# Which engine ends the program: the last wait for HBM copies moves from GpSimd to SyncE

## The chip, the cores and the metric

The kernel runs on one core of a Trainium2 chip. The metric is device time in microseconds; before the change the median of three runs is 106.08 us (105.78 to 106.34). A profile of one execution (a trace, and a page made from it) is read beside it; that execution took 106.19 us.

## The reference

A token is kept where its position is below the capacity, and set to zero otherwise:

```python
def setup_inputs():
    batch, seq, hidden, capacity = 16, 1024, 512, 256
    return {
        "x": np.random.randn(batch, seq, hidden).astype(np.float32),
        "token_positions": np.random.randint(0, capacity, (batch, seq)).astype(np.int32),
        "capacity": capacity,
    }

def reference(x, token_positions, capacity):
    mask = token_positions < capacity
    return (x * mask[..., np.newaxis]).astype(np.float32)
```

`x` has 16,384 tokens of 512 float32 numbers, 33.55 MB. The positions reach the chip as 64-bit integers, and the kernel reads them as pairs of 32-bit words. With these inputs every position lies below the capacity, so no token is dropped and the output equals `x`.

## The kernel before

The kernel bets that nothing is dropped, and repairs the output if something was.

**The copies.** Lines 77 to 83 issue eight copies from `x` to `out`, HBM to HBM, of 4 MB each, in turn from SyncE (`sp`) and ScalarE (`act`). Each adds 16 to the semaphore `s_copy` when it has landed, one from each DMA engine, so all eight are done at 128. ScalarE issues the load of the token positions (line 72) ahead of its copies. Lines 86 to 95 then take these nine instructions out of their place and put them at the very start of the program, ahead of the compiler's own opening barriers, so that the copies begin at once.

**The flag.** VectorE compares the positions with the capacity (lines 103 to 117: `ge`, `lt`, `low`, `keep`, each 128 x 128), adds up each row (`kept`, line 119), TensorE adds the rows (line 123), and line 125 makes the flag `drop_i`: 1 if fewer than all tokens are kept. SyncE, ScalarE and VectorE read it into a register (line 133). If it is 1, lines 141 to 161 load all of `x` in blocks through two buffers, multiply by `keep` on VectorE and write over the copies, after waiting for `s_copy`. With these inputs the flag is 0 and the three engines jump over that part.

**The end.** Semaphores have to be at zero for the next launch. SyncE, ScalarE and VectorE each add 1 to `s_done` as they leave (lines 164 and 165; the trace files these under line 165). GpSimd (`gp`) has nothing to do until here: it waits until `s_done` is 3 (line 166), clears the range of all semaphores but `s_copy` (line 170), then waits for all eight copies (line 171) and sets `s_copy` back by 128 (line 172). Lines 171 and 172 become one instruction. It is the last of the program, and the only one that makes sure that the copies have landed.

The order of the work is written out by hand; each engine runs its own list of instructions, and nothing but semaphores ties them together. What an engine does after its last instruction of the program belongs to the runtime, not to the kernel.

Of the kernel before, what the change touches and what calls it, by code (L numbers as in the profile page):

```python
# [1 line left out]

# [4 lines left out]


@with_exitstack
def kernel(  # L10
    ctx: ExitStack,
    tc: tile.TileContext,
    x: bass.AP,
    token_positions: bass.AP,
    capacity: bass.AP,
    out: bass.AP,
):
    nc = tc.nc
    P = nc.NUM_PARTITIONS
    fp32 = mybir.dt.float32  # L20
    i32 = mybir.dt.int32
    Alu = mybir.AluOpType

    x_f = x.flatten_outer_dims()
    out_f = out.flatten_outer_dims()
    N, D = x_f.shape
    n_per_p = N // P
    cap = float(int(capacity))
    x_r = x_f.rearrange("(p n) d -> p n d", p=P)
    out_r = out_f.rearrange("(p n) d -> p n d", p=P)  # L30
    tp_i32 = token_positions.rearrange("b s -> (b s)").bitcast(i32)

    sp = nc.sync
    act = nc.scalar
    ve = nc.vector
    pe = nc.tensor
    gp = nc.gpsimd


    tc.close()  # L40
    tc.compile()  # L41

    def sbuf(name, shape, dtype):
        return ctx.enter_context(nc.sbuf_tensor(name, shape, dtype)).ap()

    tp = sbuf("tp", [P, 2 * n_per_p], i32)
    ge = sbuf("ge", [P, n_per_p], fp32)
    lt = sbuf("lt", [P, n_per_p], fp32)
    low = sbuf("low", [P, n_per_p], fp32)
    keep = sbuf("keep", [P, n_per_p], fp32)  # L50
    kept = sbuf("kept", [P, 1], fp32)
    ones = sbuf("ones", [P, 1], fp32)
    drop_i = sbuf("drop_i", [1, 1], i32)
    total = ctx.enter_context(nc.psum_tensor("total", [1, 1], fp32)).ap()
    F = 16
    NBUF = 2
    n_fix = n_per_p // F
    xts = [sbuf(f"xt{b}", [P, F, D], fp32) for b in range(NBUF)]

    s_copy = nc.alloc_semaphore("s_copy")  # L60
    s_tp = nc.alloc_semaphore("s_tp")
    s_ve = nc.alloc_semaphore("s_ve")
    s_pe = nc.alloc_semaphore("s_pe")
    s_ld = [nc.alloc_semaphore(f"s_ld{b}") for b in range(NBUF)]
    s_mul = nc.alloc_semaphore("s_mul")
    s_st = [nc.alloc_semaphore(f"s_st{b}") for b in range(NBUF)]
    s_done = nc.alloc_semaphore("s_done")

    n_copy = 0
    early = []  # L70

    load_tp = act.dma_start(out=tp, in_=tp_i32.rearrange("(p w) -> p w", p=P))
    early.append(load_tp.then_inc(s_tp, 16).ins)

    C = 16
    for k in range(n_per_p // C):
        ins = (sp, act)[k % 2].dma_start(
            out=out_r[:, k * C : (k + 1) * C, :], in_=x_r[:, k * C : (k + 1) * C, :]  # L80
        ).then_inc(s_copy, 16)
        early.append(ins.ins)
        n_copy += 1


    home = nc.cur_bb.bb
    first_bb = nc.cur_f.blocks[0]
    first_sp = next(
        k for k, i in enumerate(first_bb.instructions) if i.engine == mybir.EngineType.SP
    )  # L90
    names = [i.name for i in early]
    home.instructions = [i for i in home.instructions if i.name not in names]
    first_bb.instructions = (
        first_bb.instructions[:first_sp] + early + first_bb.instructions[first_sp:]
    )

    lo = tp[:, 0 : 2 * n_per_p : 2]
    hi = tp[:, 1 : 2 * n_per_p : 2]


    ve.memset(ones, 1.0).then_inc(s_ve, 1)  # L101
    ve.wait_ge(s_tp, 16)
    ve.tensor_scalar(  # L103
        out=ge, in0=lo, scalar1=0.0, scalar2=None, op0=Alu.is_ge
    ).then_inc(s_ve, 1)
    ve.wait_ge(s_ve, 2)
    ve.scalar_tensor_tensor(  # L107
        out=lt, in0=lo, scalar=cap, in1=ge, op0=Alu.is_lt, op1=Alu.mult
    ).then_inc(s_ve, 1)
    ve.wait_ge(s_ve, 3)  # L110
    ve.scalar_tensor_tensor(  # L111
        out=low, in0=hi, scalar=0.0, in1=lt, op0=Alu.is_equal, op1=Alu.mult
    ).then_inc(s_ve, 1)
    ve.wait_ge(s_ve, 4)
    ve.scalar_tensor_tensor(  # L115
        out=keep, in0=hi, scalar=0.0, in1=low, op0=Alu.is_lt, op1=Alu.add
    ).then_inc(s_ve, 1)
    ve.wait_ge(s_ve, 5)
    ve.tensor_reduce(  # L119
        out=kept, in_=keep, axis=mybir.AxisListType.X, op=Alu.add  # L120
    ).then_inc(s_ve, 1)
    pe.wait_ge(s_ve, 6)
    pe.matmul(out=total, lhsT=ones, rhs=kept, start=True, stop=True).then_inc(s_pe, 1)  # L123
    ve.wait_ge(s_pe, 1)
    ve.tensor_scalar(  # L125
        out=drop_i, in0=total, scalar1=float(N) - 0.5, scalar2=None, op0=Alu.is_lt
    ).then_inc(s_ve, 1)


    for e in (sp, act, ve):  # L130
        e.wait_ge(s_ve, 7)
    ET = mybir.EngineType
    drop = nc.values_load(
        drop_i[0:1, 0:1],
        engines=[ET.SP, ET.Activation, ET.DVE],
        min_val=0,
        max_val=1,
        skip_runtime_bounds_check_because="a comparison gives 0 or 1",
    )
    with nc.If(drop):  # L140
        for u in range(n_fix):
            b = u % NBUF
            if u >= NBUF:
                sp.wait_ge(s_st[b], 16 * (u // NBUF))
            sp.dma_start(out=xts[b], in_=x_r[:, u * F : (u + 1) * F, :]).then_inc(s_ld[b], 16)
            ve.wait_ge(s_ld[b], 16 * (u // NBUF + 1))
            for j in range(F):
                c = u * F + j
                ve.tensor_scalar(
                    out=xts[b][:, j, :],  # L150
                    in0=xts[b][:, j, :],
                    scalar1=keep[:, c : c + 1],
                    scalar2=None,
                    op0=Alu.mult,
                ).then_inc(s_mul, 1)
            if u == 0:
                act.wait_ge(s_copy, 16 * n_copy)
            act.wait_ge(s_mul, (u + 1) * F)
            act.dma_start(out=out_r[:, u * F : (u + 1) * F, :], in_=xts[b]).then_inc(s_st[b], 16)
        for b in range(NBUF):  # L160
            act.wait_ge(s_st[b], 16 * (n_fix // NBUF))


    for e in (sp, act, ve):
        e.sem_inc(s_done, 1)
    gp.wait_ge(s_done, 3)
    own = [s_tp, s_ve, s_pe, *s_ld, s_mul, *s_st, s_done]
    ids = sorted(s.num for s in own)
    assert ids == list(range(ids[0], ids[-1] + 1))
    gp.sem_clear(range(ids[0], ids[-1] + 1))  # L170
    gp.wait_ge(s_copy, 16 * n_copy)
    gp.sem_inc(s_copy, -16 * n_copy)


# [1 line left out]
_INS = ['x', 'token_positions', 'capacity']  # L176
_OUTS = [((16, 1024, 512), 'float32')]

_NUMBERS = {'capacity': 256}


# [26 lines left out]
```

## Time and profile before

| what | value |
|---|---|
| time, median of three runs | 106.08 us |
| time of the profiled execution | 106.19 us |
| its span, first to last instruction | 104.3 us |
| HBM read, written | 33.69 MB, 33.55 MB |
| both together over the span | 645 GB/s |
| SyncE's queue, ScalarE's queue, share of 16 DMA engines' span | 48.6%, 49.4% |
| VectorE, GpSimd, TensorE busy | 1.5, 0.2, 0.2 us |

The page gives first how long each engine was busy, then the span in 40 equal slices with a digit for each (9 is 90% busy or more) and what the DMA engines moved, then the chain of waits that ended last, the costliest groups of instructions, and the DMA issues with the median time to their landing. Engines are named PE (TensorE), DVE (VectorE), ACT (ScalarE), POOL (GpSimd) and SP (SyncE); a "q" behind the name, as in SPq or POOLq, means the engine's sequencer, which handles semaphores, branches and the issue of copies. These are not counted as busy time. An answer on one line of the kernel gives for each kind of instruction the shortest, median and longest duration in ns, and when the first and the last began, in us from the start of the span. The trace also holds a log: each change of a semaphore, with its number and time, among them semaphores that the kernel doesn't own. `s_copy` is number 99 in it, `s_done` number 108.

### The profile page before, as it was taken

The page shows a single profiled execution, that of the slowest core. Times are in us where ns is not written, and L with a number is a line of the kernel's source. Part 1 is how long each engine was busy: PE and PEld are TensorE (multiplying, and loading weights), DVE is VectorE, ACT ScalarE, POOL GpSimd, SP SyncE. Part 2 cuts the span into 40 slices and gives each one's busy share as a digit, 9 for nine tenths or more (in the row PEclk, how much of TensorE's full clock was granted, in tenths as well). Part 3 has the DMA queues.
Part 4 walks back from the last instruction along what each step waited for, and adds up shares of the span by engine and source line. Part 5 has one row for each costly group of instructions (what it writes and reads, how often), then busy time and mean ns, then how long its engine had stood idle before and what let it go on. Part 6 is the DMA issues. An engine that isn't in the chain of part 4 may idle for free. (4 is left out here: it accounts for less than half of the span.)

```text
span 104.3 us, 70 instructions
## 1 busy us (share of the span) xinstructions
PE 0.2 (0%) x2; PEld 0.1 (0%) x2; DVE 1.5 (1%) x7; POOL 0.2 (0%) x4
## 2 busy tenths in 40 slices
PE   0000000000000000000000000000000000000000
PEld 0000000000000000000000000000000000000000
DVE  0230000000000000000000000000000000000000
POOL 0000000000000000000000000000000000000000
DMA  8999989989989989999899997998997999989984
GB/s 251 402 352 302 339 280 339 339 302 352 339 289 390 314 276 377 289 327 352 289 364 327 302 377 239 377 377 289 352 327 276 377 327 314 390 276 327 364 277 163
DMA packets 1297, 33.69 MB, mean 323 GB/s; under 512 B 144, under 2 KB 272, under 8 KB 272
## 3 DMA queue, kind: packets, MB, share of 16 engines
q10 hardware_dynamic: 720, 16.91, 49.4%
q1 hardware_dynamic: 576, 16.78, 48.6%
q14 instruction: 1, 0.01, 0.0%
HBM read 33.69 MB, written 33.55 MB: 645 GB/s over the span
## 5 line engine op out<-in xcount | busy, mean ns | idle before, releaser
L107 DVE SCALAR_TENSOR_TENSOR lt<-tp,ge 128x128 f32<-128x128 int32 x1 | 0.3, 293 | 0.0
L111 DVE SCALAR_TENSOR_TENSOR low<-tp,lt 128x128 f32<-128x128 int32 x1 | 0.3, 291 | 0.0
L115 DVE SCALAR_TENSOR_TENSOR keep<-tp,low 128x128 f32<-128x128 int32 x1 | 0.3, 291 | 0.0
L119 DVE TENSOR_REDUCE kept<-keep 128x1 f32<-128x128 f32 x1 | 0.3, 286 | 0.0
L103 DVE TENSOR_SCALAR ge<-tp 128x128 f32<-128x128 int32 x1 | 0.2, 228 | 0.0
L123 PE MATMUL total<-kept,ones 128*1 128x1 f32 x2 | 0.2, 164 | 6.2 <-DVE kept L119 6.2
L125 DVE TENSOR_SCALAR drop_i<-total 1x1 int32<-1x1 f32 x1 | 0.1, 145 | 0.3 <-PE total L123 0.3
L101 DVE MEMSET ones<- 128x1 f32 x1 | 0.1, 59 | 4.6 <-PEq L41 4.6
L189 POOL MEMSET const-bfloat16-1.0<- 128x1 bf16 x1 | 0.1, 101 | 0.0
L189 POOL MEMSET const-uint8-127<- 128x1 uint8 x1 | 0.1, 101 | 0.0
L189 POOL MEMSET const-float32-0.0<- 128x1 f32 x1 | 0.1, 98 | 0.2 <-issue 0.2
L189 POOL MEMSET const-float32-1.0<- 128x1 f32 x1 | 0.1, 98 | 0.0
L123 PEld LDWEIGHTS total<-kept,ones 128*1 128x1 f32 x2 | 0.1, 80 | 6.2 <-DVE kept L119 6.2
## 6 DMA issues: line engine op xcount, KB each, us to landing
out_dram<-in_x_dram SPq DMA_DIRECT2D x4, 4096.0 KB, 62.2
out_dram<-in_x_dram ACTq DMA_DIRECT2D x4, 4096.0 KB, 68.1
tp<-in_token_positions_dram ACTq DMA_DIRECT2D x1, 128.0 KB, 2.1
```

Source lines behind the costliest of these rows:

```text
L101: ve.memset(ones, 1.0).then_inc(s_ve, 1)
L103: ve.tensor_scalar(out=ge, in0=lo, scalar1=0.0, scalar2=None, op0=Alu.is_ge).then_inc(s_ve, 1)
L107: ve.scalar_tensor_tensor(out=lt, in0=lo, scalar=cap, in1=ge, op0=Alu.is_lt, op1=Alu.mult).then_inc(s_ve, 1)
L111: ve.scalar_tensor_tensor(out=low, in0=hi, scalar=0.0, in1=lt, op0=Alu.is_equal, op1=Alu.mult).then_inc(s_ve, 1)
L115: ve.scalar_tensor_tensor(out=keep, in0=hi, scalar=0.0, in1=low, op0=Alu.is_lt, op1=Alu.add).then_inc(s_ve, 1)
L119: ve.tensor_reduce(out=kept, in_=keep, axis=mybir.AxisListType.X, op=Alu.add).then_inc(s_ve, 1)
L123: pe.matmul(out=total, lhsT=ones, rhs=kept, start=True, stop=True).then_inc(s_pe, 1)
L125: ve.tensor_scalar(out=drop_i, in0=total, scalar1=float(N) - 0.5, scalar2=None, op0=Alu.is_lt).then_inc(s_ve, 1)
L189: nc = _bacc.Bacc("TRN2", target_bir_lowering=False, num_devices=1)
```

## The change

The wait for the copies and the setting back of `s_copy` move from GpSimd to SyncE. SyncE no longer adds to `s_done` on its own, but after ScalarE and VectorE have: it waits for 2 and makes it 3. GpSimd waits for 3 as before, clears the range and has no more to do. So SyncE is the engine that ends the program, and GpSimd's last instruction comes early. It is meant to take GpSimd out of what follows the last landing.

```diff
-    for e in (sp, act, ve):
+
+    for e in (act, ve):
         e.sem_inc(s_done, 1)
-    gp.wait_ge(s_done, 3)
+    sp.wait_ge(s_done, 2)
+    sp.sem_inc(s_done, 1)
     own = [s_tp, s_ve, s_pe, *s_ld, s_mul, *s_st, s_done]
     ids = sorted(s.num for s in own)
     assert ids == list(range(ids[0], ids[-1] + 1))
+    gp.wait_ge(s_done, 3)
     gp.sem_clear(range(ids[0], ids[-1] + 1))
-    gp.wait_ge(s_copy, 16 * n_copy)
-    gp.sem_inc(s_copy, -16 * n_copy)
+    sp.wait_ge(s_copy, 16 * n_copy)
+    sp.sem_inc(s_copy, -16 * n_copy)
```

## The prediction

> **What bounds the kernel now.** I began with the page: its row of DMA business in 40 slices and its issue table.
>
> ```profile
> span 104.3 us, 70 instructions
> ...
> DMA  8999989989989989999899997998997999989984
> ...
> out_dram<-in_x_dram SPq DMA_DIRECT2D x4, 4096.0 KB, 62.2
> out_dram<-in_x_dram ACTq DMA_DIRECT2D x4, 4096.0 KB, 68.1
> tp<-in_token_positions_dram ACTq DMA_DIRECT2D x1, 128.0 KB, 2.1
> ```
>
> The DMA engines are busy from the first slice to the last, where the digit falls to 4; eight copies of 4 MB inside HBM are all they do. The page's chain of waits names only the DVE and PE work of the first 7 us: it starts from the last computing instruction and doesn't see that the end hangs on a copy. So I asked for lines 79, 170, 172 and 165 and for the last stretch.
>
> ```profile
> DMA to landing us min/median/max: 25.0/65.2/101.7
> ...
> L170 POOLq EVENT_SEMAPHORE_RANGE_CLEAR  x1: 92/92/92, 7.8 to 7.8; - x1
> ...
> L172 POOLq EVENT_SEMAPHORE  x1: 17/17/17, 104.3 to 104.3; - x1
> ...
> L165 ACTq EVENT_SEMAPHORE  x1: 17/17/17, 7.3 to 7.3; - x1
> L165 SPq EVENT_SEMAPHORE  x1: 17/17/17, 7.3 to 7.3; - x1
> L165 DVEq EVENT_SEMAPHORE  x1: 21/21/21, 7.8 to 7.8; - x1
> ```
>
> The last copy was issued by ScalarE at 2.5 us and takes 101.7 us to land, which gives 104.2 to 104.3 us. GpSimd's line 172, 17 ns long, follows at once, and the span ends with it. GpSimd's clearing of the other semaphores is at 7.8 us, and SyncE, ScalarE and VectorE have signed off by then. One landing sets the end, and one GpSimd instruction stands between it and the end of the program.
>
> The span is not the time, though: the profiled execution took 106.19 us against a span of 104.30, so 1.89 us lie outside. No view prints that part, but the trace's log of semaphore updates does. On the span's clock it reads:
>
> ```
> s_copy, last landing of 128                 104.257 us
> GpSimd's line 172 begins / ends             104.281 / 104.298
> s_copy set back                             104.306
> semaphore 2, updates 1 and 2                6.593, 7.455
> semaphore 2, updates 3 to 9                 104.859, .903, .927, 105.024, .063, .097, .144
> semaphores 207 to 255 set, first            105.043
> last of semaphores 7 to 255 set             105.716
> semaphore 2, nine updates more              105.940 to 106.297
> ```
>
> Semaphore 2 isn't the kernel's: it is a barrier of the five engines, each adding its step in turn, then every engine resets a block of about 51 semaphores, then a second barrier. Update 1 comes 0.16 us after TensorE's only matmul was signalled (at 6.433), update 2 comes 0.14 us after ScalarE's line 165 ended at 7.311. The third waited 97.4 us and came 0.561 us after GpSimd's line 172 ended. The kernel's own semaphores 105 to 108 are reset in one block beginning 105.198, 0.14 us after update 7, and the blocks begin in the order 207, 156, 105, 54 and then the lowest. From this I read the turn order TensorE, ScalarE, GpSimd, VectorE, SyncE; the last two are an inference, as no record names who added a step. All of it ends 106.297 us after the first instruction, within 0.11 us of the 106.19 measured, so I take the measured time to contain this closing work.
>
> **What the Trainium skill says.** "Runtime: NRT & Kernel Launch", section "The ~15µs preamble/postamble breakdown", has the same things after a kernel: a barrier, a reset of 51 semaphores per engine, another barrier, at 44 ns a hop. The trace agrees: the six steps from update 3 to 9 take 0.285 us, 47 ns each. Its 1.5 us for that barrier isn't what is seen: 0.846 us from the end of line 172 to update 9, of which 0.561 is ahead of update 3. "Perfetto Trace Analysis", section "Sequencer-only Instruction (DRAIN, etc)", says that such an instruction's record holds its execution and neither its wait nor the spread of its update. That agrees too: line 172 is 17 ns after a wait of 96 us, its wake-up takes 24 ns (104.257 to 104.281) and its update appears 8 ns after its end. No page prices how long an engine takes from its last instruction to its turn in the barrier, and this is what decides here.
>
> **The change, part by part.**
>
> *SyncE waits for ScalarE and VectorE, then signs off; GpSimd clears.* One semaphore instruction on SyncE becomes one with a wait. VectorE signs off last, at 7.8 us, so SyncE is released then, adds its step some 25 ns plus 17 ns later, and GpSimd's clearing (92 ns) moves from 7.83 to about 7.9 us. All of that lies under copies that run for 96 us more. Behind the new wait on SyncE stands only its next wait: its four issues are over at 2.9 us, the loads of the branch aren't run (the flag is 0), and nobody but GpSimd waits for it. Cost on the path: 0.
>
> *The wait for the copies and the setting back of s_copy move from GpSimd to SyncE.* The same instruction form, 17 ns on SyncE (line 165) as on GpSimd (line 172). The copies' issue order and queues are untouched. So the span itself shouldn't move: landing, 24 ns, 17 ns. Cost: 0 to 0.02 us.
>
> *GpSimd takes its turn in the barrier early; SyncE comes last.* Before, from the last landing: 0.024 wake + 0.017 instruction + 0.561 GpSimd's way to its turn = update 3 at +0.602; then 0.044 and 0.024 for the two turns after it: update 5 at +0.670 us. After, updates 1 to 4 should be there by about 8.6 us (GpSimd ends its clearing at about 8.0, plus 0.56, plus 0.04). Only SyncE's own is missing: 0.024 + 0.017 + its way to its turn. The trace before doesn't show that way, since SyncE was there 96 us too soon. The bounds: the nearest row is ScalarE, a sequencer with the same 17 ns semaphore instruction and the same kind of copies issued, 7.311 to 7.455 = 0.144 us; the other bound is GpSimd's 0.561. I take ScalarE's: in the compiler's barriers at line 41, SyncE's and ScalarE's DRAINs take 7 and 8 ns against GpSimd's 34 to 41, so SyncE behaves like ScalarE and GpSimd is the odd one. Update 5 at +0.041 + 0.144 = +0.185 us. Saved: 0.670 - 0.185 = 0.485 us. With GpSimd's way for SyncE it would be 0.068 us. All after update 5 (0.217 us to update 9, the reset, the second barrier) is the same.
>
> The sum: 106.08 - 0.485 = 105.595, rounded to 105.60 us, 0.46% less.
>
> **Rivals.**
>
> *SyncE's way is as long as GpSimd's, or the time ends with the program's last instruction.* Then 0.07 us or nothing is saved: 106.0 to 106.1 us. For it: 0.561 us may be the price of whichever engine wakes after a long sleep, and TensorE and ScalarE left after a short one. The profiled time is also 0.11 us short of the last barrier update, so I don't know exactly where the clock stops. Against it: 1.89 us outside the span is too near the length of the closing work (1.999 us) to be something else.
>
> *SyncE's way is still shorter than ScalarE's.* If update 5 follows like one hop (0.024 us after the instruction), it stands at +0.065 and the saving is 0.605: 105.47 us. For it: SyncE is the last in turn and all others stand ready. Against it: TensorE's 0.16 and ScalarE's 0.14 show a way even for engines whose turn had come.
>
> *SyncE's way is longer than GpSimd's: slower.* SyncE has a queue of copies and a branch behind it. Its DRAIN behind the issues at 3.0 us took 373 ns, a register load (line 133) 467 ns, a fetch of 8 KB of instructions by the DMA 324 to 493 ns in this trace. If all three stood in its closing path: 0.041 + 0.373 + 0.467 + 0.493 = +1.374 us for update 5, against +0.670: 0.70 us lost, 106.78 us. Against it: ScalarE too had issued copies and jumped past the same branch, and needed 0.144 us with its copies still under way, so nothing there drains them.
>
> **How the numbers follow.** 0.55 for the main case, 0.15 for the still shorter way, 0.20 for nothing or 0.07 us, 0.10 for slower. Copies add their own spread: the three runs before lie from 105.78 to 106.34, half a microsecond for one program, so a median of a few can be off by about 0.2 us. The bound of faster, 0.5%, is 105.55 us and the main case is 0.05 us above it: I give half of it, and a little more, to faster (0.30 of 0.55), and nearly all of the still shorter way (0.14); with 0.03 from the rest, faster is 0.47. Same is the rest of the main case and most of the null one: 0.43. Slower is 0.10. The range reaches from 105.47 less 0.3 of spread, some 105.15, to 106.1 plus 0.2 of spread, 106.30; the slower case is left out.
>
> **What would show it.** In the changed kernel: the copy row unchanged, the last semaphore instruction on SyncE about 24 ns after the last landing, GpSimd's clearing near 7.9 us. In the log, semaphore 2's third and fourth updates near 8.6 us and its fifth 0.15 to 0.25 us after the last landing. If that gap is 0.6 us or more, I was wrong on SyncE's way; if it is short and the time is unmoved, the clock doesn't contain it. If the copies' landing itself moves by more than 0.3 us, neither explains the time.

## The result, and the profile after

The changed kernel takes 105.51 us (median of six runs, 105.24 to 105.64) against 106.05 us before (median of six): the ratio is 0.9948, with a 95% interval of 0.9926 to 0.9970. That is 0.54 us less, where the prediction had 0.485. The copies alone spread the six runs before over 0.56 us, so the size is better read behind the last landing, further down.

The page of the changed kernel, its first line, its row of DMA business in 40 slices and its issues with the median time to landing:

```profile
span 103.9 us, 70 instructions
...
DMA  7998999979989899799899899997998998989974
...
out_dram<-in_x_dram SPq DMA_DIRECT2D x4, 4096.0 KB, 61.9
out_dram<-in_x_dram ACTq DMA_DIRECT2D x4, 4096.0 KB, 67.7
tp<-in_token_positions_dram ACTq DMA_DIRECT2D x1, 128.0 KB, 2.2
```

The copies fill the span as before, from the same queues in the same sizes. Next come the answers on the lines of the end (line 166 holds the sign-offs of ScalarE and VectorE, 168 that of SyncE, 173 GpSimd's clearing, 175 the setting back of `s_copy`), and the landings of the copies of line 79. EVENT_SEMAPHORE is the instruction that waits for a semaphore, changes one, or both:

```profile
DMA to landing us min/median/max: 24.5/64.8/101.4
...
L166 ACTq EVENT_SEMAPHORE  x1: 17/17/17, 7.3 to 7.3; - x1
L166 DVEq EVENT_SEMAPHORE  x1: 21/21/21, 7.8 to 7.8; - x1
...
L168 SPq EVENT_SEMAPHORE  x1: 17/17/17, 7.8 to 7.8; - x1
...
L173 POOLq EVENT_SEMAPHORE_RANGE_CLEAR  x1: 92/92/92, 7.9 to 7.9; - x1
...
L175 SPq EVENT_SEMAPHORE  x1: 17/17/17, 103.9 to 103.9; - x1
```

SyncE signs off once VectorE has, GpSimd clears at 7.9 us, and no instruction of the program begins from there until SyncE's line 175, which ends the span. The span is 0.4 us shorter in this execution, because the last copy landed earlier (at 103.867 us of the span against 104.257). The record gives no sign that the change did that: over the six runs the span lies between 103.9 and 104.3 us, as the copies happen to land.

The trace's log of semaphore updates has what is gained. Semaphore 2 is that of the two closing barriers, with nine updates each; all times are in us after the last landing of a copy, but "early" ones, which are on the span's clock:

```
                                       before            changed
last instruction begins / ends         0.024 / 0.041     0.017 / 0.034
semaphore 2, early updates             6.593, 7.455      6.615, 7.479, 8.500, 8.543
semaphore 2, next updates              0.602 (3rd)       0.165 (5th)
semaphore 2, 5th, 6th, 9th update      0.670 .767 .887   0.165 .209 .329
last of the semaphores reset           1.459             0.901
last update of the second barrier      2.040             1.482
```

From the last landing to the last update that the closing leaves in the log, the changed kernel needs 0.558 us less: 0.505 of it by the fifth update, 0.053 between the fifth and the ninth, nothing after.

### The profile page after: what moved, and what is told of

It is laid out like the page before. It is cut to its first block, busy times and chain, and to the rows that moved or that the text cites. A ratio compares the mean times of both kernels' runs of the same rounds, so it can differ in the third digit from the quotient of the medians.

```text
span 103.9 us, 70 instructions
## 1 busy us (share of the span) xinstructions
PE 0.2 (0%) x2; PEld 0.1 (0%) x2; DVE 1.5 (1%) x7; POOL 0.2 (0%) x4
```

## The experiments

My theory was this: the time ends with the runtime's closing work, in which the five engines take turns in the order TensorE, ScalarE, GpSimd, VectorE, SyncE. What counts is how long the engine that ends the program takes from its last instruction to its turn (its "way"), and how many turns come after. The rivals: an engine that slept through 96 us of copies is slow in going on, whichever it is; the gain is in who notices the landing; or the chained sign-off has a part in it.

Besides the log there is a second reading that the copies' spread doesn't touch: each run's time less its own span, the mean over the runs. Before, it is 1.88 us in both sets below (57 and 33 runs, 1.84 to 1.94, spans being on record to 0.1 us); in the six runs of the result after the change it is 1.32 us (1.29 to 1.34).

The experiments ran in two sets, e1 to e4 on one chip and e5 to e7 on another. The kernel before takes 105.60 us in the first set and 105.16 in the second, against 106.05 beside the result. The times expected in e1 to e4 reckon from the 106.05, so only their differences can be compared.

| run | who ends | time, median | before beside it | ratio, interval | time less span |
|---|---|---|---|---|---|
| before | GpSimd | | | | 1.88 |
| changed | SyncE | 105.51 | 106.05 | 0.9948 (0.9926 to 0.9970) | 1.32 |
| e1 | SyncE, old sign-off | 105.00 | 105.60 | 0.9937 (0.9917 to 0.9956) | 1.31 |
| e2 | ScalarE | 105.29 | 105.60 | 0.9960 (0.9944 to 0.9975) | 1.50 |
| e3 | VectorE | 105.28 | 105.60 | 0.9969 (0.9953 to 0.9985) | 1.47 |
| e4 | GpSimd, SyncE waits | 105.77 | 105.60 | 1.0013 (1.0001 to 1.0025) | 1.85 |
| e5 | SyncE, the change again | 104.70 | 105.16 | 0.9958 (0.9934 to 0.9983) | 1.33 |
| e6 | TensorE | 104.94 | 105.16 | 0.9974 (0.9958 to 0.9990) | 1.68 |
| e7 | SyncE, eight set-backs | 105.08 | 105.16 | 0.9996 (0.9980 to 1.0013) | 1.33 |

The log of each profiled execution, in us after the last landing ("early" updates are those of the first closing barrier that came 95 us or more before it):

| run | who ends | early updates | last instruction ends | way | ninth update |
|---|---|---|---|---|---|
| before | GpSimd | 2 | 0.041 | 0.561 | 0.887 |
| changed, e1, e5 | SyncE | 4 | 0.034 | 0.131 | 0.329 |
| e2 | ScalarE | 1 | 0.038 | 0.144 | 0.505 |
| e3 | VectorE | 3 | 0.049 | 0.182 | 0.472 |
| e4 | GpSimd | 2 | 0.233 | 0.526 | 1.044 |
| e6 | TensorE | 0 | 0.080 | 0.274 | 0.715 |
| e7 | SyncE | 4 | 0.451 | 0.136 | 0.750 |

**e1: the wait moves, the sign-off stays.** Against the kernel before:

```diff
     gp.sem_clear(range(ids[0], ids[-1] + 1))
-    gp.wait_ge(s_copy, 16 * n_copy)
-    gp.sem_inc(s_copy, -16 * n_copy)
+    sp.wait_ge(s_copy, 16 * n_copy)
+    sp.sem_inc(s_copy, -16 * n_copy)
```

> Only the last wait moves to SyncE; the sign-off stays as before the change (SyncE, ScalarE and VectorE each add 1 to s_done at once). Theory (the gain is the way of the ending engine to its turn in the closing barrier): as the changed kernel, the barrier's fifth update 0.165 us and its ninth 0.33 us after the last landing, about 105.5 us. Rival (the chained sign-off has a part in the gain or a cost of its own): the ninth update differs from 0.33 us by over 0.05.

The barrier's updates stand 0.165, 0.209, 0.247, 0.282 and 0.329 us after the last landing, each the same to the nanosecond as in the changed kernel. The chained sign-off neither brings nor costs anything that the log shows; the moved wait is the whole gain.

**e2 and e3: ScalarE or VectorE ends.** As e1, with `act` or `ve` in place of `sp` in the two new lines. Against the kernel before, with e3's engine in a comment that isn't in the kernels:

```diff
-    gp.wait_ge(s_copy, 16 * n_copy)
-    gp.sem_inc(s_copy, -16 * n_copy)
+    act.wait_ge(s_copy, 16 * n_copy)        # e3: ve
+    act.sem_inc(s_copy, -16 * n_copy)       # e3: ve
```

> ScalarE makes the last wait and sets s_copy back; the rest as in the run with SyncE. Theory with the turn order TensorE, ScalarE, GpSimd, VectorE, SyncE: one update of the barrier (TensorE's) early, the second 0.04 + 0.144 = 0.185 us after the last landing, then steps of 0.038, 0.044, 0.024 and 0.217 to the ninth at 0.51 us; about 105.7 us. Rival 1 (an engine that slept through the copies needs GpSimd's 0.56 us, SyncE alone excepted): second update at 0.60, ninth at 0.93 us, about 106.1 us. Rival 2 (place in the turn order plays no part): ninth at 0.33 us as with SyncE, 105.5 us.

> VectorE makes the last wait and sets s_copy back; the rest as in the run with SyncE. Theory: three updates of the barrier early, the fourth about 0.21 us after the last landing (0.045 for wake and instruction, 0.164 for a way a quarter longer than SyncE's 0.131, as its semaphore instruction is 21 ns against 17), fifth 0.235, ninth 0.45 us; about 105.6 us. Rival 1 (sleep costs 0.56 us): fourth at 0.61, ninth at 0.85 us, about 106.05 us. If the turn order read from the log is wrong, the number of early updates isn't three.

The answer on line 174, where the setting back stands, in e2:

```profile
L174 ACTq EVENT_SEMAPHORE  x1: 17/17/17, 104.0 to 104.0; - x1
```

and in e3:

```profile
L174 DVEq EVENT_SEMAPHORE  x1: 21/21/21, 103.7 to 103.7; - x1
```

These instructions end 0.038 and 0.049 us after the last landing. With ScalarE one update is early, the second comes at 0.182 us, so ScalarE's way is 0.144 us, the number it had before after a short wait. With VectorE three are early and the fourth comes at 0.231, a way of 0.182 (0.164 expected). The ninth stands at 0.505 and 0.472, expected 0.51 and 0.45. Both rivals to e2 fall: an engine that has slept through the copies isn't slow for that, and the place in the order does cost. Of the 0.176 us that e2's ninth update is later than SyncE's, 0.105 are the three turns from the second update to the fifth and 0.054 come between the fifth and the ninth; 0.017 are ScalarE's own. Of e3's 0.143 us, 0.024 and 0.053 are of those two kinds, and 0.066 are VectorE's own slower wake-up, instruction and way.

**e4: SyncE waits, GpSimd ends.** Against the changed kernel:

```diff
     for e in (act, ve):
         e.sem_inc(s_done, 1)
-    sp.wait_ge(s_done, 2)
+    sp.wait_ge(s_copy, 16 * n_copy)
+    sp.sem_inc(s_copy, -16 * n_copy)
     sp.sem_inc(s_done, 1)
+    gp.wait_ge(s_done, 3)
...
-    gp.wait_ge(s_done, 3)
     gp.sem_clear(range(ids[0], ids[-1] + 1))
-    sp.wait_ge(s_copy, 16 * n_copy)
-    sp.sem_inc(s_copy, -16 * n_copy)
```

> SyncE waits for the copies and sets s_copy back, and only then signs off; GpSimd clears the range after that, so GpSimd ends the program though it no longer waits for a copy. Theory: two updates of the barrier early, the third after two semaphore instructions on SyncE (0.07), GpSimd's wake and clearing (0.03 + 0.092) and its way of 0.526 us as seen behind its clearing in the changed kernel, 0.72 us after the last landing, ninth at 1.0 us; about 106.15 us, 0.1 above the kernel before. Rival (GpSimd was slow in noticing the landing, and the gain is in who waits): third update at 0.3 us, ninth at 0.6 us, about 105.75 us.

The answers on SyncE's two instructions (lines 169, 170) and on GpSimd's clearing (175):

```profile
L169 SPq EVENT_SEMAPHORE  x1: 17/17/17, 104.1 to 104.1; - x1
...
L170 SPq EVENT_SEMAPHORE  x1: 17/17/17, 104.2 to 104.2; - x1
...
L175 POOLq EVENT_SEMAPHORE_RANGE_CLEAR  x1: 92/92/92, 104.2 to 104.2; - x1
```

SyncE notices the landing as in the changed kernel, 0.017 us after it, and all of the gain is lost: GpSimd's clearing ends 0.233 us after the landing, the third update comes at 0.759, the ninth at 1.044 (0.72 and 1.0 expected). The way is 0.526 us, and the kernel is 0.13% slower than before, with 0.01 to 0.25% as the interval. So the gain isn't in who waits for the copies but in who ends the program.

**e5 and e6: the change again, and TensorE ends.** e5 is the changed kernel itself. e6 is e1 with TensorE:

```diff
-    gp.wait_ge(s_copy, 16 * n_copy)
-    gp.sem_inc(s_copy, -16 * n_copy)
+    pe.wait_ge(s_copy, 16 * n_copy)
+    pe.sem_inc(s_copy, -16 * n_copy)
```

> The changed kernel once more, beside the others of this set. Theory: the closing again 0.33 us from the last landing to the barrier's ninth update and 1.48 us to the last of the second barrier, 0.55 us below the kernel before, as in the run with the old sign-off (ratio 0.9937 there).

> TensorE makes the last wait and sets s_copy back. Theory: TensorE is first in turn, so all nine updates of the barrier come after the last landing: the first at 0.24 us (0.024 wake, 0.051 for its longer semaphore instruction, 0.16 way), then 0.034, 0.038, 0.044 and 0.024 to the fifth at 0.38 and 0.217 more to the ninth at 0.59 us; about 0.3 us below the kernel before and 0.26 above the changed one. If the first turn isn't TensorE's, some update stands early, at 6 to 9 us, as in all runs so far.

e5 repeats the closing (ninth update 0.329 us, last one of all 1.481). Its median is 0.46 us under the kernel before, where 0.55 was expected; the interval takes in 0.55. In e6 no update is early, so the first turn is TensorE's, and with one, two, three and four early ones in e2, e4, e3 and e5 the order of the turns is settled. The answer on e6's setting back:

```profile
L174 PEldq EVENT_SEMAPHORE  x1: 51/51/51, 103.0 to 103.0; - x1
```

It ends 0.080 us after the landing; the first update follows at 0.354, so TensorE's way is 0.274 us where I had expected 0.16 (the distance from its matmul's signal before). The ninth comes at 0.715 in place of 0.59. Why the way is longer behind a semaphore instruction than behind a matmul stays open. In the time e6 is 0.22 us under the kernel before and 0.24 over the change.

**e7: the same end, more of it.** Against the changed kernel:

```diff
-    sp.sem_inc(s_copy, -16 * n_copy)
+    for _ in range(n_copy):
+        sp.sem_inc(s_copy, -16)
```

> The changed kernel, but SyncE sets s_copy back in eight steps of 16 in place of one of 128, so seven semaphore instructions more stand between the last landing and SyncE's turn. In the run where SyncE waited and GpSimd ended, two such instructions began 0.082 us apart. Theory: the barrier's fifth update at 0.165 + 7 x 0.082 = 0.74 us, the ninth at 0.90, the time 0.57 us above the changed kernel, at that of the kernel before within 0.1. Rival (the measured time ends with the landing or doesn't contain the closing work): unmoved against the changed kernel.

The page's first line and the answer on the line of the set-backs:

```profile
span 104.1 us, 77 instructions
...
L176 SPq EVENT_SEMAPHORE  x8: 17/17/17, 103.7 to 104.1; - x8
```

Seven instructions more, and the last begins 0.434 us after the landing where the first begins at 0.017: on the mean 0.060 us apart (0.057 to 0.065), not the 0.082 seen between two different semaphores in e4. The fifth update is at 0.587 and the ninth at 0.750 (0.74 and 0.90 expected): 0.42 us more than in e5. The time rises by 0.38 us over e5 by the medians (0.50 by the means; e5 has six runs) and can't be told from the kernel before. So what is put behind the last landing is paid for, and the measured time doesn't end with the landing. The set-backs are part of the program, though, and lie inside the span. That the time contains the closing behind the program as well is seen in the two tables together: in every row the time less span is 1.01 to 1.05 us more than what lies between the end of the last instruction and the ninth update. In all nine profiled executions (before, changed, e1 to e7), besides, the measured time is 0.107 to 0.114 us less than the distance from the first instruction to the last update of the second barrier.

All five engines have now ended the program. SyncE closes soonest, with the least way and the last of the five turns, and e1 and the changed kernel close alike; no version beat them.

## Why the prediction was right

The path that it named, from the last landing through the ending engine to its turn in the barrier, is the one that got shorter. One step of it was costed wrongly, and one reason for its main number doesn't hold.

- *The bound.* A landing sets the end, with one instruction behind it: right. In the two profiled executions the last landing moved by 0.39 us, more than the 0.3 that I had set as a sign against reading the time, so this pair's times settle nothing. Beside each other in the set of e5 the spans agree, with means of 103.33 us before and 103.28 changed (33 and 6 runs).
- *Edits costed at nothing.* The chained sign-off: right by e1, to the nanosecond. The wake-up and the instruction: SyncE wakes 0.017 us after the landing against GpSimd's 0.024, a gain of 0.007 us that I had not counted.
- *SyncE's way.* I took ScalarE's 0.144 us, between 0.561 and one hop of 0.024. It is 0.131 us (0.165 less 0.034). That choice carried the forecast, and e2 shows why it served: ScalarE's way is 0.144 us after the long wait too, and GpSimd's is 0.526 (behind its clearing, after 3.4 us of wait in the changed kernel and after nearly 100 us in e4) or 0.561 (behind the set-back). For these two engines the way goes with the engine, not with the sleep; the others were seen behind a semaphore instruction after a long wait only.
- *"All after update 5 is the same."* This step failed, by 0.053 us. From the fifth to the ninth update it took 0.217 us before and 0.164 after. The difference is one step, fifth to sixth: 0.097 against 0.044. The sixth comes 0.121 or 0.122 us after the *fourth* in the kernel before, e2, e3, e4 and e6, in which the fourth came only after the landing, and the steps after it are alike. In e5, e1 and e7 the fourth was there 95 us ahead and the sixth follows the fifth by 0.043 or 0.044 us. If VectorE takes the sixth step on the way back, it has to get from its first turn to its second, and SyncE's end hides that. The second closing barrier speaks for it: there all nine updates come after the landing in every run, and the sixth comes 0.121 to 0.123 us after the fourth and 0.098 to 0.100 after the fifth, in the kernels that SyncE ends too. Still this reading is argued from the times; no record names who added a step.
- *The sum.* Forecast 0.485; by the log 0.558: 0.505 to the fifth update (0.013 from SyncE's way and 0.007 from its wake-up are what I missed) and the 0.053. By time less span 0.55 to 0.57 us, by the medians 0.54 and, in e5, 0.46.
- *The rivals.* Nothing gained: out, by the 0.56 us between the readings of time less span. Slower by SyncE's long way: out; nothing of drain, load or fetch stands in 0.131 us. The still shorter way of 0.024: out as a way, though its saving of 0.605 us lies nearer to the log's 0.558 than the main case's 0.485: the 0.053 and the small misses made up for the way.

How much of it was luck? My reason for giving SyncE a way like ScalarE's was the length of their DRAINs, and it doesn't hold. The answer on line 41 of the kernel before has all five engines:

```profile
L41 SPq DRAIN  x3: 7/7/7, 3.9 to 4.3; - x3
L41 POOLq DRAIN  x2: 34/38/41, 3.9 to 4.2; - x2
L41 ACTq DRAIN  x2: 8/8/8, 3.9 to 4.3; - x2
L41 DVEq DRAIN  x2: 10/10/10, 4.0 to 4.3; - x2
L41 PEldq DRAIN  x2: 8/8/8, 4.0 to 4.3; - x2
```

TensorE's DRAINs are as short as ScalarE's and VectorE's nearly so, yet their ways are 0.274 and 0.182 us (e6, e3). So a short DRAIN doesn't tell of a short way, and that SyncE's came so near to ScalarE's was luck as far as this reason goes. Everything that I missed saved time (0.007, 0.013 and 0.053 us), and the sum of it is small beside the 0.56 us over which the six runs before lie.

The Trainium skill's "Runtime: NRT & Kernel Launch", section "The ~15µs preamble/postamble breakdown", has the first closing barrier at some 1.5 us. Here it is 0.295 us from the end of SyncE's last instruction to the ninth update and 0.846 from GpSimd's; the measurement decides. The 44 ns a hop that the prediction quotes stand in that section's row of the opening barrier, not of the closing one. The nine updates of semaphore 2 just ahead of the first instruction of the kernel before take 0.371 us, 46 ns a step, and the six steps at the end 47 ns each; single steps run from 23 to 113 ns.

## What to carry to other kernels

Behind the last instruction of this kernel there is still a closing of 1.4 to 2 us, all but about 0.11 of it in the measured time, and its length depends on which engine comes last. Where another kernel's last wait is GpSimd's, let SyncE make it and let GpSimd leave early: that was worth 0.56 us here, half a percent of 105 us. It was tried on this kernel alone. To see such a thing, compare the time with the span, then read the log of semaphore updates behind the last instruction; the page and its chain of waits end too soon.

## What the runs showed of the hardware that I had not expected

- GpSimd needs 0.526 us from the end of its clearing to its turn, after a short wait as after a long one, and 0.561 from the end of its set-back; SyncE needs 0.131 (0.136 behind eight set-backs), ScalarE 0.144, VectorE 0.182, TensorE 0.274 behind a semaphore instruction. What GpSimd does in that time no record shows.
- Semaphore instructions of 17 ns on SyncE begin on the mean 0.060 us apart when they change one semaphore and 0.082 us apart in the one pair that changed two different ones.
- In neither closing barrier of the nine traces did the sixth update come sooner than 0.121 us after the fourth, and the engine that ends last decides whether that shows.
